# One streaming encoder layer: the scores matrix held in four places, reused by both projections, and PE alone in hand-written order in the down-projection

## The chip, the core and the metric

The kernel runs on one core of one Trainium2 chip. The metric is the device time of one execution in microseconds (us). TensorE (PE) does the matrix products, VectorE (DVE), ScalarE (ACT) and GpSimd (POOL) the work on elements, and SyncE (SP) issues most transfers; POOL issues the stores of intermediate results.

## What is computed

One layer of a streaming encoder for 2112 tokens (2048 of a prompt, 64 of a sample), width 1024, in fp32:

```
x = x + rms_norm(token_mixer(rms_norm(x)))        # gated convolution and mLSTM
x = x + rms_norm(memory_attend(rms_norm(x)))      # 4 heads, 256 memory tokens
x = x + rms_norm(conv_ffn(rms_norm(x)))

def conv_ffn(xn, ff_buf, w_up, ffn_conv_w, w_down):
    up, ff_new = causal_dwconv(xn @ w_up, ff_buf, ffn_conv_w)
    a, g = jnp.split(up, 2, axis=-1)
    return (jax.nn.gelu(g) * a) @ w_down, ff_new
```

`w_up` is 1024 x 5632 and `w_down` 2816 x 1024. The gains of the norms are folded into operands where that is possible.

## The kernel before

Every fp32 operand of a product is split into a high part, cast by ACT to the matrix format (L103), and a low part, which DVE subtracts (L104); `split` does both. A product of two operands is then three products on PE (`mm3`, L117 high by high, L118 and L119 with one low part). A profile row of line 103 or 104 is thus named by its tile alone.

The program has five phases. Phases 1 and 2 are the token mixer. Phase 3 is the attention: the weights of queries and keys are multiplied into one scores matrix `A`, those of values and output into `B`, both kept in SBUF with high and low parts. Tokens come in 16 chunks of 128 (and the sample's 64): scores `sc` from `A`, softmax `pp`, transposes into `ps`, then `yo` from `B`, the post-norm (`post`, L553) to `yn`, and the transpose of the next norm's input (`x2_T`, tiles `xr` and `tp`, L1238), stored as `x2T`.

Phase 4 is the up-projection, a Strassen-Winograd form with seven products instead of eight. Tokens come in three passes of two column blocks of 352, and each pass goes over 22 values of f: 66 units. A unit has seven products of four pairs (84 instructions of PE): the weights `wa`, `wb`, `wc`, `wd` (partly sums made earlier and kept in `wsd`) by the token operands B11, T2, B21, T1, T3, T4, B22, which DVE makes from the four quarters R11, R12, R21, R22 of `x2T`; X is R22 - R12 after R12 has become R12 - R11. `head1` is the first product of a unit, `head2` the second. Results are convolved, passed through gelu and stored by POOL as `hd`.

Phase 5 is the down-projection in six parts of 3, 3, 4, 4, 4, 4 blocks of 128 rows of `w_down`. A part loads and splits its weights (`load_down`: tiles `raw`, then `dh` and `dl`), and goes over nine groups of tokens, of 256 (one of 64): `load_h` loads `hr` from `hd` and splits it to `hh`, one group ahead (`need(i + 1)`), PE makes `y`, and DVE adds it to the accumulator of its tile `acc`. In the last part each tile of 128 tokens also gets the post-norm: two squares on ACT, a multiplication by the gain on POOL, small steps `poss`, `pov`, `por`, the addition of the residual `xt` (L570), and two stores `out_y`, which SP issues.

The order of instructions on an engine is either the scheduler's or that of the program. In phases 3 to 5 PE and SP have the order in which the code is written (`self.ms`), in the last part of phase 5 ACT, DVE and POOL too. SP issues in its order, and a transfer that must wait for a buffer or a result holds back those behind it. `raw` has three buffers; `hr`, `hh` and `xt` have two each.

Of the kernel before, what the change touches and what calls it, by code (L numbers as in the profile page):

```python
# [35 lines left out]
HEAD = 120  # L36
# [31 lines left out]
class Prog:  # L68
# [68 lines left out]
    def build(self):  # L137
        tc, nc = self.tc, self.nc
        with ExitStack() as es:
# [35 lines left out]
            self.pe = mybir.EngineType.PE  # L175
            self.zes = es.enter_context(ExitStack())
# [803 lines left out]
    def phase3(self):  # L980
# [4 lines left out]
        ap = self.pool(self.zes, "za").tile([P, 2, KT, D], F32R, name="A")  # L985
        bp = self.pool(self.zes, "zb").tile([P, 2, KT, D], F32R, name="B")
        A = lambda part, k, sl: ap[:, part, k, sl]
        B = lambda part, k, sl: bp[:, part, k, sl]
        with ExitStack() as es:
# [203 lines left out]
            for i in range(16):  # L1193
# [17 lines left out]
                if i + 1 < 16:  # L1211
                    pT(ch[i + 1])
                next(y)
# [28 lines left out]


    def phase4(self):
# [11 lines left out]
        KH = KT // 2  # L1256
        self.zes.close()
        self.zes = ExitStack()
        with ExitStack() as es:
# [6 lines left out]
            def t_op(n):  # L1266
                pool = right if n in ("T3", "B21") else left
                return pool.tile([P, KH, 2, NB], F32R, tag=n, name=n, bufs=1)

            def t_raw(n):  # L1270
                return left.tile([P, KH, NB], F32, tag=n, name=n, bufs=1)

            def w_op(n, bufs=1):
                return left.tile([P, 2, 2, KH, P], F32R, tag=n, name=n, bufs=bufs)


            ops = {n: t_op(n) for n in ("B11", "T2")}
            raws = {n: t_raw(n) for n in ("R11", "R12", "R21", "R22")}
            first = {n: w_op(n) for n in ("wa", "wb")}
            X = early.tile([P, KH, NB], F32, tag="X", name="X", bufs=1)  # L1280
# [9 lines left out]
            def w_load(u, part=("wa", "wb"), w=None):  # L1290
# [3 lines left out]
                if "wa" in part:  # L1294
                    w = W()
                    w.u, w.r = u, {}
                    w.r["wa"] = self.raw(a["w_up"][f], (P, KT, P)).rearrange("p (two k) c -> p two k c", two=2)
                if "wb" not in part:
                    return w
# [3 lines left out]
                w.r["wd"] = right.tile([P, KH, P], F32, tag="wr1", name="wr1", bufs=2)  # L1303
# [4 lines left out]
            def w_split(w, n):  # L1308
                if w is None:
                    return  # L1310
                if n == "wd":
                    o = left.tile([P, 2, KH, P], F32R, tag="wd", name="wd", bufs=1)
                else:
                    o = first.pop(n, None)
                    if o is None:
                        o = w_op(n, 2 if n == "wc" else 1)
                self.split(o[:, 0], o[:, 1], w.r[n])
                w.o[n] = o

            class Tk:  # L1320
                pass

            def t_load(p):
                t = Tk()
                t0 = 2 * NB * p
                t.r = raws if p == 0 else {n: t_raw(n) for n in ("R11", "R12", "R21", "R22")}
                t.w = None
                for n in ("R11", "R21", "R12", "R22"):
                    k0, c0 = (int(n[1]) - 1) * KH, t0 + (int(n[2]) - 1) * NB
                    self.dma(t.r[n], self.x2T[k0:k0 + KH, :, c0:c0 + NB].rearrange("k p t -> p k t"))  # L1330
                    if p == 0 and t.w is None:
                        t.w = w_load(0, ("wa",))
                t.o = {}
                t.X = X if p == 0 else None
                return t

            def t_split(p, t, n, src):
                o = ops[n] if p == 0 and n in ops else t_op(n)
                self.split(o[:, :, 0], o[:, :, 1], src)
                t.o[n] = o  # L1340

            def t_adds(t):
                V.tensor_tensor(out=t.r["R12"], in0=t.r["R12"], in1=t.r["R11"], op=ALU.subtract)
                if t.X is None:
                    t.X = early.tile([P, KH, NB], F32, tag="X", name="X", bufs=1)
                V.tensor_tensor(out=t.X, in0=t.r["R22"], in1=t.r["R12"], op=ALU.subtract)

            def t_t3(t):
                V.tensor_tensor(out=t.r["R11"], in0=t.X, in1=t.r["R11"], op=ALU.subtract)

            def t_t4(t):
                V.tensor_tensor(out=t.r["R21"], in0=t.r["R21"], in1=t.X, op=ALU.subtract)

            def prod(pt, w, n, i, o, more=False):
                h, l = (w.o[n][:, j] if i is None else w.o[n][:, j, i] for j in range(2))
# [47 lines left out]
            def head1(u, w, o):  # L1403
# [5 lines left out]
                v.p1 = vt("p1")  # L1409
# [10 lines left out]
            tk = t_load(0)  # L1420
            w = w_load(0, ("wb",), tk.w)
            with tc.high_priority(offset=HEAD):
                w_split(w, "wa")
                t_split(0, tk, "B11", tk.r["R11"])
                t_adds(tk)
                t_split(0, tk, "T2", tk.X)
            v = head1(0, w, tk.o)
            t_split(0, tk, "B21", tk.r["R21"])
            w_split(w, "wb")
            head2(v, tk.o)  # L1430
            t_split(0, tk, "T1", tk.r["R12"])
# [258 lines left out]
```

## Time and profile before

| | |
|---|---|
| median of 3 runs | 2946.56 us (2938.88 to 2947.24) |
| the profiled execution's own time | 2947.28 us |
| its span, first to last instruction | 2945.6 us |
| mean granted clock of PE | 0.989 |
| busy: PE, DVE, ACT, POOL | 2846.5, 1716.3, 1206.6, 378.0 us |
| instructions of PE | 15906 |

The span is what the rows of the trace cover; the time of an execution has 1.7 us around it. The median differs from the profiled execution by 0.7 us. A busy share is a mean over phases that have different limits, so the stretches around each change of phase have to be read by themselves.

### The profile page before, as it was taken

How to read it: one execution, taken by the hardware profiler on the slowest of the kernel's cores; microseconds unless marked ns; L12 is line 12 of the kernel's file. 1: busy time of each engine (PE TensorE's matmuls, PEld its weight loads, DVE VectorE, ACT ScalarE, POOL GpSimd, SP SyncE). 2: the span in 40 equal slices, each digit the busy share in tenths (PEclk: the TensorE clock that was granted, in tenths of full speed). 3: DMA queues.
4: the chain of work that ended last, by engine and by line, in shares of the span. 5: the costliest groups of instructions: out<-in, count | busy, mean ns of one | idle time of the engine just before them, and what ended most of it. 6: DMA issues, size and time to landing. Idle time of an engine off the chain costs nothing.

```text
span 2945.6 us, 41739 instructions
## 1 busy us (share of the span) xinstructions
PE 2846.5 (97%) x15906; PEld 2628.0 (89%) x15906; DVE 1716.3 (58%) x2815; ACT 1206.6 (41%) x2463; POOL 378.0 (13%) x608
## 2 busy tenths in 40 slices
PE   8999999999999999999979999999999989999987
PEld 8999999998988877788779999999999988888875
DVE  6413422355666555666477778877877753443457
ACT  5224223234344443223256566656666653110122
POOL 1111011112212202222100000000000000000034
PEclk9999999999999999999989999999999999999998
DMA  8434332158666335777455544554454532221235
GB/s 277 149 98 134 99 112 94 57 159 278 219 206 219 127 108 172 235 257 241 152 176 201 168 157 167 194 173 157 156 174 154 174 109 82 84 73 45 82 120 164
DMA packets 211498, 456.84 MB, mean 155 GB/s; under 512 B 25414, under 2 KB 113672, under 8 KB 211298
## 3 DMA queue, kind: packets, MB, share of 16 engines
q1 hardware_dynamic: 180418, 346.14, 37.2%
q0 software_dynamic: 28720, 100.17, 8.9%
q10 hardware_dynamic: 2160, 7.87, 1.0%
q8 instruction: 125, 2.05, 0.3%
q14 instruction: 75, 0.61, 0.1%
HBM read 345.56 MB, written 108.54 MB: 154 GB/s over the span
## 4 chain that ended last, share of the span: by engine, by line
PE 51%; DVE 6%; DMA 4%; issue 2%; ACT 1%; SPq 1%; POOL 0%; DVEq 0%; POOLq 0%; ACTq 0%
PE up L117 10%; PE up L119 10%; PE up L118 10%; PE y L118 4%; PE y L119 4%; PE y L117 4%; DMA sums<-in_w_up 2%; DVE acc L570 1%; PE yo L117 1%; PE yo L118 1%; PE yo L119 1%; DMA hr<-hd 1%; PE sc L119 1%; PE sc L117 1%; PE sc L118 1%
## 5 line engine op out<-in xcount | busy, mean ns | idle before, releaser
L117 PE MATMUL y<-dh,hh 128*128 128x512 f32 x704 | 278.9, 396 | 20.5 <-ACT hh L103 15.4
L119 PE MATMUL y<-dh,hh 128*128 128x512 f32 x704 | 278.7, 396 | 2.4 <-DVE hh L104 2.3
L118 PE MATMUL y<-dl,hh 128*128 128x512 f32 x704 | 277.7, 394 | 2.4 <-DVE dl L104 2.4
L117 PE MATMUL mm<-xs,wh 128*128 128x384 f32 (+2 forms) x768 | 249.0, 324 | 10.3 <-ACT xs L109 7.5
L119 PE MATMUL mm<-xs,wl 128*128 128x384 f32 (+2 forms) x768 | 248.7, 324 | 1.0 <-DVE wl L104 1.0
L118 PE MATMUL mm<-xs,wh 128*128 128x384 f32 (+2 forms) x768 | 248.8, 324 | 0.0
L1589 DVE TENSOR_TENSOR acc<-y,acc 128x512 f32<-128x512 f32 x170 | 115.7, 689 | 179.8 <-PE y L119 176.9
L117 PE MATMUL up<-B,wa 128*128 128x352 f32 x528 | 172.5, 327 | 8.8 <-ACT wa L103 8.8
L117 PEld LDWEIGHTS y<-dh,hh 128*128 128x128 f32 x704 | 134.7, 191 | 51.1 <-ACT hh L103 17.9
L117 PE MATMUL up<-T,wb 128*128 128x352 f32 x528 | 172.4, 326 | 3.7 <-ACT wb L103 2.6
L119 PE MATMUL up<-B,wa 128*128 128x352 f32 x528 | 170.3, 323 | 3.2 <-DVE wa L104 3.2
L117 PE MATMUL mmb<-bh,xs 128*128 128x384 f32 (+1 forms) x512 | 173.4, 339 | 0.0
L119 PE MATMUL mmb<-bh,xs 128*128 128x384 f32 (+1 forms) x512 | 172.5, 337 | 0.0
L118 PE MATMUL mmb<-bl,xs 128*128 128x384 f32 (+1 forms) x512 | 172.4, 337 | 0.0
L118 PE MATMUL up<-T,wb 128*128 128x352 f32 x528 | 170.3, 322 | 2.0 <-DVE T L104 2.0
L103 ACT CAST hh<-hr 128x1024 fp32r<-128x1024 f32 (+3 forms) x54 | 49.4, 914 | 297.5 <-PE y L119 248.8
L118 PE MATMUL up<-B,wa 128*128 128x352 f32 x528 | 170.7, 323 | 0.1
L119 PE MATMUL up<-T,wb 128*128 128x352 f32 x528 | 169.7, 321 | 0.5 <-DVE wb L104 0.5
L119 PEld LDWEIGHTS y<-dh,hh 128*128 128x128 f32 x704 | 134.5, 191 | 33.5 <-DVE hh L104 5.6
L118 PEld LDWEIGHTS y<-dl,hh 128*128 128x128 f32 x704 | 134.5, 191 | 31.1 <-DVE dl L104 3.1
L76 POOL DMA_DIRECT2D hd<-da x88 | 47.5, 541 | 851.1 <-DVE da L1491 822.8
L117 PEld LDWEIGHTS mm<-xs,wh 128*128 128x128 f32 x768 | 145.8, 190 | 10.7 <-ACT xs L109 7.5
(462 smaller groups left out, 7853.4 us busy)
## 6 DMA issues: line engine op xcount, KB each, us to landing
ws<-wsd SPq DMA_DIRECT2D x132, 512.0 KB, 4.3
raw<-in_w_up SPq DMA_DIRECT2D x66, 512.0 KB, 5.4
raw<-in_wA SPq DMA_DIRECT2D x47, 512.0 KB, 3.6
sums<-in_w_up SPq DMA_DIRECT2D x176, 128.0 KB, 4.1
wsd<-sums POOLq DMA_DIRECT2D x44, 512.0 KB, 4.2
wr<-in_w_up SPq DMA_DIRECT2D x66, 256.0 KB, 4.6
xt<-in_x SPq DMA_DIRECT2D x32, 512.0 KB, 4.4
hr<-hd SPq DMA_DIRECT2D x32, 512.0 KB, 3.9
```

The lines of the kernel that those rows point to most:

```text
L76: self.nc.gpsimd.dma_start(out=out, in_=in_)
L103: nc.scalar.copy(hi, src)
L117: nc.tensor.matmul(out, lhsT=lh, rhs=rh, start=(first and i == 0), stop=False, skip_group_check=more)
L118: nc.tensor.matmul(out, lhsT=lh, rhs=rl, start=False, stop=False, skip_group_check=more)
L119: nc.tensor.matmul(out, lhsT=ll, rhs=rh, start=False, stop=(last and i == n - 1), skip_group_check=more)
L570: nc.vector.scalar_tensor_tensor(out=yn[:w, sl], in0=yn[:w, sl], scalar=r[:w, 0:1], in1=xt[:w, sl], op0=ALU.mult, op1=ALU.add)
L1589: V.tensor_tensor(out=acc[j][:, sl], in0=pt, in1=acc[j][:, sl], op=ALU.add)
```

## The change

The scores matrix `A` is four tiles of [128, 2, 2, 1024] instead of one, in a pool of its own (`za`) that stays open to the end of the kernel. Their four places are used again twice. In phase 4 they hold `Z0` to `Z3`: B11 and T2 in split form with the high and low parts of `wa`, the four quarters, X (in two pieces, three and one of its four blocks) and p1. In phase 5 they hold the weights: parts 0, 2 and 4 in A2 and A3, the others in A0 and A1, and `hh5`, the first group's `hh`, in A0.

`head4`, called in the loop of phase 3, issues the loads of R11, of the first raw weights and of R12, R22, R21 after the last scores, and later in two steps the splits of `wa` and R11, the subtractions, and the split of T2. `head5`, called in the last three units of phase 4, loads and splits the first weights of the down-projection and its first group. Phase 5 no longer stands in `self.ms`; it has a manual order for PE alone, and in the last part still one for ACT, DVE and POOL. The weights of the next part are loaded ahead of `need(i)` in the loop. `wr1` has one buffer instead of two.

```
@@ phase 3
-        ap = self.pool(self.zes, "za").tile([P, 2, KT, D], F32R, name="A")
+        self.za = self.pool(self.zaes, "za")
+        ap = [self.za.tile([P, 2, 2, D], F32R, tag="A%d" % i, name="A%d" % i, bufs=1) for i in range(4)]
...
+                if i == 14:
+                    self.head4(0)
                 y = yout(ch[i])
                 next(y)
+                if i == 14:
+                    self.head4(1)
...
+                if i == 15:
+                    self.head4(2)
                 next(y)
+    def head4(self, step):
+        nc, V = self.nc, self.nc.vector
+        if step == 0:
+            z = [self.za.tile([P, 4 * D], F32R if i < 2 else F32, tag="A%d" % i, name="Z%d" % i, bufs=1) for i in range(4)]
...
+            self.t_load4(0, ("R11",))
+            self.w4 = self.raw(self.a["w_up"][0], (P, KT, P)).rearrange("p (two k) c -> p two k c", two=2)
+            self.t_load4(0, ("R12", "R22", "R21"))
+        elif step == 1:
+            o = self.ops4["B11"]
+            self.split(self.wa4[0], self.wa4[1], self.w4)
+            self.split(o[:, :, 0], o[:, :, 1], self.raw4["R11"])
+        else:
+            self.t_adds4()
+            o = self.ops4["T2"]
+            for x, ks in self.X4:
+                self.split(o[:, ks, 0], o[:, ks, 1], x)
@@ phase 4
-                w.r["wd"] = right.tile([P, KH, P], F32, tag="wr1", name="wr1", bufs=2)
+                w.r["wd"] = right.tile([P, KH, P], F32, tag="wr1", name="wr1", bufs=1)
...
+            def head5(step):
+                if step == 0:
+                    self.dn = self.load_down(0, ("A2",), 0, 2)
...
+                    self.dma(self.hr5.rearrange("p (f t) -> p f t", f=PARTS[0]),
+                             self.hd[0:PARTS[0], :, 0:2 * P].rearrange("f p t -> p f t"))
+                else:
+                    t = self.za.tile([P, 4 * D], F32R, tag="A0", name="hh5", bufs=1)
...
+                    self.split(self.hh5[:, 0], self.hh5[:, 1], self.hr5.rearrange("p (f t) -> p f t", f=PARTS[0]))
+                    self.dn += self.load_down(0, ("A3",), 2)
...
+                if u == len(units) - 3:
+                    head5(0)
...
                 w_split(n, "wc")
+                if n is None:
+                    head5(1)
@@ phase 5
             with ExitStack() as self.ms:
                 self.phase3()
                 self.phase4()
-                self.phase5()
+            self.phase5()
...
+            es.enter_context(tc.manual_schedule(engines={self.pe}))
...
-            with tc.high_priority(offset=HEAD):
-                need(0)
-                ws = {0: load_down(0, 0, PARTS[0])}
+            hs[0] = self.hh5
+            ws = {0: self.dn}
...
+                if t0 == groups[3] and pi + 1 < len(PARTS):
+                    ws[pi + 1] = self.load_down(pi + 1, ("A2", "A3") if pi % 2 else ("A0", "A1"))
...
                 need(i)
                 need(i + 1)
-                if t0 == groups[3] and pi + 1 < len(PARTS):
-                    ws[pi + 1] = load_down(pi + 1, f0s[pi + 1], PARTS[pi + 1])
```

The order of PE and of POOL is the same in both kernels. Three places on other engines differ as follows. The first is ACT from phase 3 into phase 4: L560 (before) and L561 are the squares of the post-norm, L1128 (before) and L1130 the square for `xr`, B11 and Z0, T2 and Z1 the split operands. Before:

```order
L560 ACTIVATE pp_13084,poss_13556<-yo3_13531 128x512
L1128 ACTIVATE xr_13476,ss2_13569<-yn3_10175 128x1024
L560 ACTIVATE pp_13288,poss_13642<-yo3_13576 128x512
L560 ACTIVATE pp_13288,poss_13642<-yo3_13601 128x512
L1128 ACTIVATE xr_13628,ss2_13655<-yn3_10175 128x1024
L1367 COPY ca_13749<-halo_13693 128x2
L1367 COPY cg_13835<-halo_13693 128x2
L1367 COPY ca_13891<-halo_13693 128x2
L103 CAST B11_13684<-R11_13686 128x4x352
L103 CAST wa_13690<-raw_13697 128x1024
L103 CAST B21_13731<-R21_13688 128x4x352
L1410 COPY p1_13729<-up_13716 128x352
```

In the changed kernel, over the same squares (the casts of B11 and `wa`, here of `Z0`, stand four and three rows above the first one shown):

```order
L103 CAST ps3_13290<-tp_13541 128x512
L103 CAST Z1_13480<-Z2_13481 128x3x352
L561 ACTIVATE pp_13087,poss_13573<-yo3_13548 128x512
L103 CAST Z1_13480<-Z3_13482 128x352
L1130 ACTIVATE xr_13489,ss2_13586<-yn3_10178 128x1024
L561 ACTIVATE pp_13291,poss_13666<-yo3_13593 128x512
L561 ACTIVATE pp_13291,poss_13666<-yo3_13625 128x512
L1130 ACTIVATE xr_13652,ss2_13679<-yn3_10178 128x1024
L1430 COPY Z3_13482<-up_13716 128x352
L103 CAST B21_13730<-Z3_13482 128x4x352
L103 CAST wb_13733<-ws_13710 128x1024
```

The casts of B11 and `wa` have moved ahead of the squares of the last two chunks and the two casts of T2 between them; that of B21 still follows the last square (`xr_13652`), now behind the copy of p1 (L1430, which writes Z3).

The second is SP's queue from phase 4 into phase 5: `raw` are weights of the down-projection and `hr` groups of `hd`. Before:

```order
L73 DMA wr_22448<-in_w_up 128x512
L73 DMA hr<-hd 128x3x256
L73 DMA raw<-in_w_down 128x1024 x3
L73 DMA hr<-hd 128x3x256 x3
L73 DMA raw<-in_w_down 128x1024 x3
L73 DMA hr<-hd 128x3x256 x3
```

In the changed kernel:

```order
L73 DMA wr_22319<-in_w_up 128x512
L73 DMA raw<-in_w_down 128x1024 x2
L73 DMA hr_22330<-hd 128x3x256
L73 DMA raw<-in_w_down 128x1024 x5
L73 DMA hr<-hd 128x3x256 x2
```

Two weight tiles now stand ahead of the first group's `hr`, and five more between it and those of the next groups.

The third is SP's queue in the last part: `out_y<-acc` with the tile's number behind it are the stores of a tile (the first is 22831 before, 22715 after), `xt` the residual of a later tile, `hr` a group. Before:

```order
L73 DMA hr<-hd 128x4x256
L73 DMA xt_25400<-x2d 128x1024
L73 DMA out_y<-fo_25382 64x512 x2
L73 DMA xt_25444<-x2d 128x1024
L73 DMA out_y<-acc_22831 128x512 x2
L73 DMA hr<-hd 128x4x256
L73 DMA xt_25493<-x2d 128x1024
L73 DMA out_y<-acc_22832 128x512 x2
L73 DMA xt_25537<-x2d 128x1024
L73 DMA out_y<-acc_22833 128x512 x2
L73 DMA hr<-hd 128x4x256
L73 DMA xt_25586<-x2d 128x1024
```

In the changed kernel:

```order
L73 DMA hr<-hd 128x4x256 x4
L73 DMA out_y<-fo_25215 64x512 x2
L73 DMA xt_25277<-x2d 128x1024
L73 DMA out_y<-acc_22715 128x512 x2
L73 DMA xt_25326<-x2d 128x1024
L73 DMA hr<-hd 128x4x256
L73 DMA out_y<-acc_22716 128x512 x2
L73 DMA xt_25370<-x2d 128x1024
L73 DMA out_y<-acc_22717 128x512 x2
L73 DMA xt_25419<-x2d 128x1024
L73 DMA hr<-hd 128x4x256
L73 DMA out_y<-acc_22718 128x512 x2
```

Between the loads of `hr` stand two tiles' stores in either order, but before the change two such loads stand ahead of the first stores in this last part, and after it four (the row with x4 is the row ahead of `out_y<-fo`), so that each later load stands four tiles of stores earlier.

## Rows read from the trace of the kernel before

**Rows 1.** The waits of PE, whole kernel: us in total, times, longest.
```profile
PE y L117 <- ACT hh L103: 15.4, 6, 4.1
```

**Rows 2.** Windows by stretch: busy us (instructions) of each engine, granted clock, DMA.
```profile
1479.00:1505.00 26.00, 11.54 (x38) 9.71 (x38) 20.48 (x21) 14.67 (x19) 2.73 (x5) 0.67 0.37 123
2300.00:2390.00 90.00, 90.00 (x564) 90.00 (x564) 68.20 (x93) 54.27 (x124) 6.44 (x12) 1.00 0.37 122
2420.00:2800.00 380.00, 380.00 (x1678) 314.63 (x1678) 150.39 (x188) 70.14 (x86) 0.00 (x0) 1.00 0.24 73
```

**Rows 3.** Timeline of PE, phase 3 into 4: start, us, instruction, [idle before <-releaser].
```profile
1475.27 1.03 PE L1238 MATMUL tp<-ident,xr 128*128 128x128 f32 x8
...
1478.65 0.39 PE L119 MATMUL yo<-B,ps 128*128 128x512 f32 x1
...
1487.87 0.66 PE L117 MATMUL up<-B,wa 128*128 128x352 f32 x1 [8.83 <-ACT wa L103]
...
1498.31 0.66 PE L117 MATMUL up<-T,wb 128*128 128x352 f32 x1 [2.63 <-ACT wb L103]
...
1504.99 0.32 PE L117 MATMUL up<-T,wc 128*128 128x352 f32 x1
```

**Rows 4.** DMA issues: tiles, count, size, median us from issue to landing.
```profile
raw<-in_w_down SPq DMA_DIRECT2D x22, 512.0 KB, 5.7
...
R<-x2Td SPq DMA_DIRECT2D x12, 704.0 KB, 9.7
...
hr<-hd SPq DMA_DIRECT2D x16, 384.0 KB, 3.3
```

**Rows 5.** Timeline of ACT in the same stretch.
```profile
1483.00 1.06 ACT L1128 ACTIVATE xr<-yn 128x1024 f32<-128x1024 f32 x1 [3.17 <-DVE yn L570]
```

**Rows 6.** Timeline of DVE in the same stretch.
```profile
1473.32 0.75 DVE L1130 TENSOR_SCALAR xr<-yn,r2r 128x1024 f32<-128x1024 f32 x1 [0.75 <-POOL r2r L97]
...
1486.91 1.63 DVE L104 TENSOR_TENSOR B<-R,B 128x1408 fp32r<-128x1408 f32 x1 [1.04 <-ACT B L103]
```

**Rows 7.** Timeline of PE, phase 4 into 5.
```profile
2395.18 0.32 PE L119 MATMUL up<-B,wc 128*128 128x352 f32 x1
...
2400.62 0.80 PE L117 MATMUL y<-dh,hh 128*128 128x512 f32 x1 [5.12 <-ACT dh L103]
...
2403.76 0.80 PE L118 MATMUL y<-dl,hh 128*128 128x512 f32 x1 [2.35 <-DVE dl L104]
...
2409.38 0.39 PE L119 MATMUL y<-dh,hh 128*128 128x512 f32 x1
```

**Rows 8.** Timeline of SP's queue, phase 4 into 5.
```profile
2392.86 14.38 SPq L73 DMA_DIRECT2D hr<-hd  x3
```

**Rows 9.** Timeline of DVE in the last part.
```profile
2823.57 1.99 DVE L104 TENSOR_TENSOR hh<-hr,hh 128x1024 fp32r<-128x1024 f32 x1 [0.15 <-ACT hh L103]
...
2835.23 0.15 DVE L95 TENSOR_SCALAR pov<-poss 128x1 f32<-128x1 f32 x1
...
2840.05 1.22 DVE L104 TENSOR_TENSOR hh<-hr,hh 128x1024 fp32r<-128x1024 f32 x1 [4.66 <-ACT hh L103]
...
2850.94 0.16 DVE L95 TENSOR_SCALAR pov<-poss 128x1 f32<-128x1 f32 x1
...
2920.30 1.23 DVE L104 TENSOR_TENSOR hh<-hr,hh 128x1024 fp32r<-128x1024 f32 x1 [4.93 <-ACT hh L103]
```

**Rows 10.** Timeline of SP's queue, then of ACT, in the last part.
```profile
2850.20 0.39 SPq L73 DMA_DIRECT2D hr<-hd  x1
...
2855.06 1.04 ACT L103 CAST hh<-hr 128x1024 fp32r<-128x1024 f32 x1 [6.70 <-DMA hr<-hd]
```

**Rows 11.** Timeline of DVE, then of ACT, late in phase 4.
```profile
2341.97 0.69 DVE L104 TENSOR_TENSOR wd<-wr,wd 128x512 fp32r<-128x512 f32 x1 [2.18 <-ACT wd L103]
...
2356.32 1.05 ACT L103 CAST wa<-raw 128x1024 fp32r<-128x1024 f32 x1 [0.16 <-PE up L119]
```

**Rows 12.** Timeline of POOL in the last part.
```profile
2842.77 3.22 POOL L564 TENSOR_TENSOR acc<-acc,gpost 128x512 f32<-128x512 f32 x2 [6.70 <-ACT junk L560]
```

More of the change, by code (lines that the diff above doesn't have):

```diff
@@ L1266, in t_op @@
             def t_op(n):
+                if n in self.ops4:
+                    return self.ops4[n]
                 pool = right if n in ("T3", "B21") else left
                 return pool.tile([P, KH, 2, NB], F32R, tag=n, name=n, bufs=1)
-            def t_raw(n):
-                return left.tile([P, KH, NB], F32, tag=n, name=n, bufs=1)
             def w_op(n, bufs=1):
[L1274 to L1280, printed above, removed]
+                t = left.tile([P, 2, 2, KH, P], F32R, tag=n, name=n, bufs=bufs)
+                return t[:, 0], t[:, 1]
+            raws = self.raw4
             halo = right.tile([P, 2 * NF, 2], F32, name="halo")
@@ L1312, in w_split @@
                     o = left.tile([P, 2, KH, P], F32R, tag="wd", name="wd", bufs=1)
+                    o = o[:, 0], o[:, 1]
                 else:
[L1314 to L1317, printed above, removed]
+                    o = self.wa4 if n == "wa" else w_op(n, 2 if n == "wc" else 1)
+                self.split(o[0], o[1], w.r[n])
                 w.o[n] = o
-            class Tk:
-                pass
@@ L1323, in t_load @@
[L1323 to L1335, printed above, removed]
@@ L1348, in t_t3, with t_split, t_t2 @@
[L1348 to L1352, printed above, removed]
+            def t_split(t, n, src):
+                t[n] = o = t_op(n)
+                self.split(o[:, :, 0], o[:, :, 1], src)
+            def t_t2(t):
+                t["T2"] = o = t_op("T2")
+                for x, ks in self.X4:
+                    self.split(o[:, ks, 0], o[:, ks, 1], x)
@@ L1354, in prod, with t_t3, t_t4 @@
+            def t_t3():
+                for x, ks in self.X4:
+                    V.tensor_tensor(out=raws["R11"][:, ks], in0=x, in1=raws["R11"][:, ks], op=ALU.subtract)
+            def t_t4():
+                for x, ks in self.X4:
+                    V.tensor_tensor(out=raws["R21"][:, ks], in0=raws["R21"][:, ks], in1=x, op=ALU.subtract)
             def prod(pt, w, n, i, o, more=False):
-                h, l = (w.o[n][:, j] if i is None else w.o[n][:, j, i] for j in range(2))
+                h, l = (w.o[n][j] if i is None else w.o[n][j][:, i] for j in range(2))
@@ L1470, in phase4 @@
                 if last:
[L1471 to L1473 removed]
+                    t_split(nt, "T3", raws["R11"])
+                    t_t4()
+                on = nt if last else o
                 vn = head1(u + 1, n, on) if n else None
@@ L1505, in phase4, with load_down @@
         self.qes.close()
+    def load_down(self, pi, tags, lo=0, hi=None):
+        f0, nf = sum(PARTS[:pi]), PARTS[pi]
+        ws = []
+        for i in range(lo, nf if hi is None else hi):
+            if i % 2 == 0:
+                t = self.za.tile([P, 2, 2, D], F32R, tag=tags[(i - lo) // 2], name="dh", bufs=1)
+            raw = self.raw(self.a["w_down"][f0 + i])
+            self.split(t[:, i % 2, 0], t[:, i % 2, 1], raw)
+            ws.append((t[:, i % 2, 0], t[:, i % 2, 1]))
+        return ws
     def phase5(self):
@@ L1521, in phase5 @@
             junk = ev.tile([P, 512], F32, name="junk5")
-            def load_down(pi, f0, nf):
-                ws = []
-                pool = w1 if pi % 2 else w0
-                for i in range(nf):
-                    raw = self.raw(a["w_down"][f0 + i])
-                    wh = pool.tile([P, D], F32R, tag="h%d" % i, name="dh", bufs=1)
-                    wl = pool.tile([P, D], F32R, tag="l%d" % i, name="dl", bufs=1)
-                    self.split(wh, wl, raw)
-                    ws.append((wh, wl))
-                return ws
             def load_h(f0, nf, t0):
```

98 lines of the change are left out of this document (50 added, 48 removed).

## The prediction

> **What bounds the kernel now.** I read the waits of TensorE (PE) first, because it is the busiest engine, then the stretches at the three places where its largest waits of the up- and down-projection fall. Three sums stand out: 15.4 us in six pieces where the down-projection waits for ScalarE's (ACT) cast of `hh` [rows 1], one piece of 8.83 us for `wa` at the start of the up-projection [rows 3], and one of 5.12 us for `dh` at the start of the down-projection [rows 7]. Away from those places PE is the bound: in [rows 2] it is busy for all of 2300 to 2390 and of 2420 to 2800 at full clock, with 90.0/564 = 0.160 us for a product of the up-projection and 380.0/1678 = 0.2265 us for one of the down-projection. Nothing done to another engine in those stretches moves the end unless it makes PE wait. So the change is worth what it gives back at three places, less what it newly delays.
>
> Around a restart the waits are not the whole loss. The clock granted from 1479 to 1505 is 0.67 [rows 2], so products run at the lower of the two levels (1.2 GHz rather than 2.4 GHz) for some time after PE has stood still. I therefore price each place by the time from the last product before it to the first one after it that is undisturbed, less the products in between at full rate.
>
> **First place, scores to up-projection.** The last product of phase 3 starts at 1478.65 (so its successor could start at 1478.88), the first of `up` at 1487.87, the second weight block at 1498.31, and the third block at 1504.99 [rows 3]. Between 1478.88 and 1504.99 lie 36 products, 36 x 0.160 = 5.8 us; 20.3 us are lost. The changed kernel issues the loads of R11, of the first weights and of R12, R22, R21 as soon as the last product of scores has read the matrix, with the output products of two chunks still to come, 48 each, 2 x 48 x 0.2265 = 21.7 us, against a median landing of 9.7 us [rows 4]. B11, T2 and `wa` are then ready when PE gets there, and the first 12 products follow without a wait.
>
> What is not gained: the next 12 need B21, and in the order of ACT (shown with the change) its cast stands behind the square of the last chunk and a copy of p1. That square runs at 1483.00 for 1.06 us [rows 5], 5.2 us after 1478.88 at its end. The copy of 352 columns and the cast of 1408 are, at the square's 1.06 us for 1024, an estimated 0.4 and 1.5 us, so B21's high part is there 7 to 8 us after the end of phase 3, and its low part (1.63 us on VectorE (DVE) [rows 6]) 1.6 us later, about 9.5. PE has then stood for some 7 us, so 23 products (11 of B21, 12 of T2) run at first at the low rate, 20 of them at about twice 0.160 us less what the faster end of the stretch saves, 6.1 us in all, to the third block: 15.6 us after phase 3's end. The same instant now lies 26.1 us after it. Gain 10.5 us.
>
> Against that, the added work sits ahead of the last two chunks on DVE: two low parts, two subtractions and the split of T2, 1.63 + 1.22 + 3 x 1.6 = 7.7 us by [rows 6] and [rows 9], of which all but the last pieces, about 5.7 us, come ahead of the chain that ends in `xr` at 1473.32 + 0.75 [rows 6]; PE takes that tile for its transposes at 1475.27 without waiting [rows 3], 1.2 us later. That cover and the 0.75 us that DVE idles ahead of `xr` take up 2 us; other idle pieces of the chain may take up the rest: phase 3 ends 0 to 4 us later, I take 2.5. **Gain 8 us**, between 2 (4 us of delay, and T2 late as well) and 12 (no delay).
>
> **Second place, up- to down-projection.** The last `up` starts at 2395.18, the first `y` at 2400.62, the second at 2403.76, and the fifteenth, where full rate is back, at 2409.38 [rows 7]. 14 x 0.2265 = 3.2 us of work lies in 2409.38 - 2395.34 = 14.0: 10.8 us are lost. The first weights and `hh` now come during the last three units, and ACT and DVE have the room (in [rows 2] DVE is busy 68.2 and ACT 54.3 of 90 us). What is late next is the `hh` of the second group: needed 36 x 0.2265 = 8.15 us after 2395.34, at 2403.5 (its low part at 2403.95). On SP its load stands behind seven loads of weights, the last of which needs a buffer that is free only after a split at about 2395.5; the load then issues near 2396 and takes 3.3 us or a little more [rows 4], and its cast stays behind ACT's last work on `da`, which the added cast of `dh` pushes back by some 2.5 us, because its raw tile takes 5.7 us to land [rows 4]. I get 2401.3 to 2402.5 for the high part, 2403.3 to 2405 for the low one: a wait of 0 to 1 us. **Gain 9.5 us**, between 4 and 10.8.
>
> **Third place, the last part of the down-projection.** There DVE works in blocks of one group: a low part of `hh` starts at 2840.05 and the block ends at 2850.94 + 0.16 = 2851.10, which is 11.05 us; the next low part does not follow until the next group's cast, and the last of the six repeats starts at 2920.30 [rows 9]. (2920.30 - 2840.05)/5 = 16.05 us: 5.0 us of each repeat are idle. What ends them is the load: ACT's cast at 2855.06 waited 6.70 us for the transfer of `hr`, which SP issued at 2850.20 [rows 10]. In SP's hand-written order that load stands behind the `out_y` pairs of the group before. In the new order (shown with the change) the same load stands ahead of four more tiles of output, over 20 us earlier, so it has landed long before. DVE's block then sets the pace: it beats PE's 48 x 0.2265 = 10.9 us. The low part of the third group can start where its predecessor's block ends, 2835.23 + 0.15 = 2835.4 instead of 2840.05, and the last one at 2835.4 + 5 x 11.05 = 2890.6 instead of 2920.30. That is 29.7 us; **gain 29.5 us**. Lower bound: if each of six low parts takes 1.99 us as at 2823.57 instead of 1.22 [rows 9], 25. Upper: 31, if the first group gains too.
>
> **Costed at nothing.** The one buffer of `wr1` (two before): its load now waits for the low part of `wd`, until 2341.97 + 0.69 = 2342.7, and with it the raw weights behind it on SP, which ACT casts at 2356.32 [rows 11]. At a landing of 5.7 us they are there by 2348.4, 8 us before; if that cover were gone, each of 64 units would pay the excess. Splitting X in two adds some twelve DVE instructions and three casts in three pass changes; at full cover nothing, without it under 2 us. I deduct 0.3. The order of PE and of GpSimd (POOL) is the same row by row.
>
> **Sum.** 8 + 9.5 + 29.5 - 0.3 = 46.7 us. From the profiled execution's own 2947.28 us that gives 2900.6; the median of the runs shown lies 0.7 us lower: 2900 us, with a span near 2899.
>
> **A rule against it.** In the last part POOL multiplies for 3.22 us per tile [rows 12], and the row at 2823.57 shows a low part at 1.99 us where the one at 2840.05 takes 1.22 [rows 9]. The Trainium skill, "SBUF — State Buffer", section "Who interferes with whom", says that a VectorE instruction with two SBUF inputs and a GpSimd one that reads SBUF exclude each other for the whole instruction. The trace agrees in direction, with 1.99 us beside 1.22. By the rule, were every low part to meet a multiply and wait it out, the sum would be 35.4 us instead of 46.7.
>
> **Rivals.**
> *POOL collision.* Each of seven low parts waits out one multiply (3.22/2 = 1.6 us): 29.5 - 11.3, so about 2911 us. For it: low parts now start when POOL has long been idle, and the change moves them to the end of a block. Against it: POOL's multiply of the block's first tile ends at 2842.77 + 3.22 = 2845.99 [rows 12], before the small results that close that tile, and the second runs in the same rhythm, so that POOL is through when the next low part begins. One in ten. This is the mechanism that the section named above would make of it.
> *The second group is late at the start of the down-projection.* If the seven weight loads hold SP for longer than I reckon, PE waits up to 8 us there and pays the low clock again: the second gain is gone, 2910 us. For it: today three loads of `hr` hold SP for 14.38 us right there [rows 8], since buffers are missing. Fifteen in a hundred.
> *The last part keeps its pace.* If the load of `hr` finds its own buffer taken, or `xt` takes its place as the late transfer, 0 to 5 us remain of 29.5: 2925 to 2929 us. Against it: the buffer is freed by a low part two groups earlier. One in ten.
> *Slower.* The single `wr1` buffer makes PE wait in each unit: to end 0.3% above before it must cost (46.7 + 8.8)/64 = 0.87 us per unit, that is, SP's wait must exceed its cover of 8 us by that much. The times in [rows 11] leave it well short, but loads of `ws` stand on the same queue. Four in a hundred.
>
> **How the numbers follow.** My forecast gets 0.61, with 2890 to 2907 for its own bounds, from the sums of the bounds taken half together. Adding collision and late group takes the range to 2911 and part of the unmoved tail: 2887 to 2922. About 0.3% (9 us) is what a measurement of this kernel tells from no change; the case between, several losses at once that leave under 9 us, gets 0.03.
>
> **What would show it.** Right: `up` starts within 1 us of the last `yo`, then a wait of about 7 us for B21; `y` follows `up` without a gap; low parts of `hh` in the last part 11 us apart, the sum of waits for `hh` near nothing. Wrong: PE waits spread over the units for `wa` or `wd`; a gap over 3 us some 8 us into the down-projection; low parts still 16 us apart, or 12 to 13 with each one longer; or phase 3's last products more than 4 us later relative to its start.

## The result, and the profile after

The changed kernel takes 2900.14 us (median of 4 runs, 2897.68 to 2903.74), the kernel before 2943.83 us (4 runs, 2938.88 to 2947.24): a ratio of 0.9854, 95% interval 0.9834 to 0.9874. The forecast was 2900 us. The profiled execution took 2897.68 us, with a span of 2895.9 us (2945.6 before); it is the fastest of its four, that of the kernel before the slowest of its four. One execution in this study, of 3129.25 us in the kernel with the load moved, ran at a mean granted clock of 0.847 instead of 0.992 and is left out of its median.

PE's share rises to 98%, though it is busy for 14 us less, in line with a mean granted clock of 0.994 instead of 0.989: fewer products run at the low clock. The page's first part and PE's longest waits of the changed kernel (in total, times, longest):

```profile
PE 2832.6 (98%) x15906; PEld 2622.4 (91%) x15906; DVE 1717.6 (59%) x2827; ACT 1204.7 (42%) x2466; POOL 384.0 (13%) x608
```

```profile
PE tp L1246 <- DVE xs L104: 13.2, 8, 4.8
PE up L117 <- ACT B L103: 9.2, 1, 9.2
...
PE up L117 <- ACT u L1486: 3.2, 5, 1.3
...
PE y L119 <- DVE hh L104: 0.2, 1, 0.2
```

The 15.4 us of [rows 1] are gone, and so are the waits for `wa` and `dh` at the starts of the two projections; one wait of 9.2 us, for B21 (here `B`), has come in their place. PE's timeline from phase 3 into 4, which answers to [rows 3], and the windows of the three places, which answer to the first row of [rows 2] (first column after the stretch: its length, then PE's busy time; the third number from the end is the granted clock):

```profile
1474.63 0.39 PE L119 MATMUL yo<-B,ps 128*128 128x512 f32 x1
1474.86 0.32 PE L117 MATMUL up<-Z 128*128 128x352 f32 x1
...
1486.12 0.66 PE L117 MATMUL up<-B,Z 128*128 128x352 f32 x1 [9.19 <-ACT B L103]
1487.78 0.66 PE L118 MATMUL up<-B,Z 128*128 128x352 f32 x1 [1.00 <-DVE B L104]
...
1492.90 0.32 PE L117 MATMUL up<-T,wc 128*128 128x352 f32 x1
```

```profile
1475.00:1501.00 26.00, 15.81 (x88) 15.15 (x87) 18.13 (x21) 15.74 (x23) 1.82 (x4) 0.80 0.47 161
2385.70:2400.00 14.30, 14.30 (x65) 11.87 (x64) 9.17 (x11) 8.53 (x14) 2.15 (x4) 1.00 0.85 269
2798.20:2895.90 97.70, 87.22 (x385) 71.88 (x383) 90.16 (x111) 32.28 (x76) 66.22 (x49) 0.97 0.64 202
```

`up` follows the last `yo` at once. After 12 products PE stands for 9.19 us, and the clock falls (products of 0.66 us behind the wait, 0.32 ahead of it; 0.80 on average over the 26 us). The down-projection begins without a gap (2385.64 the last `up`, 2385.80 the first `y`) and at full clock. In the last part DVE's low parts of `hh` are 11.0 us apart:

```profile
2815.67 1.22 DVE L104 TENSOR_TENSOR hh<-hr,hh 128x1024 fp32r<-128x1024 f32 x1
...
2826.67 1.23 DVE L104 TENSOR_TENSOR hh<-hr,hh 128x1024 fp32r<-128x1024 f32 x1
...
2837.66 1.22 DVE L104 TENSOR_TENSOR hh<-hr,hh 128x1024 fp32r<-128x1024 f32 x1
```

**Where the time went.** PE executes the same 15906 products in the same order in all kernels of this study, so the same product can be found in each trace. The stages below run between the starts of five of them: the last `yo`, the first product of the third weight block of `up`, the last `up`, the fifteenth `y`, the first `y` of the last part's first full group, the last `y`; then to the end of the span. All in us, each from the profiled execution.

| kernel | last `yo` to third block | to last `up` | to 15th `y` | to last part | last part | to the end |
|---|---|---|---|---|---|---|
| before | 26.34 | 890.18 | 14.21 | 408.48 | 115.49 | 12.22 |
| changed | 18.28 | 892.74 | 3.34 | 409.24 | 86.81 | 10.92 |
| difference | -8.1 | +2.6 | -10.9 | +0.8 | -28.7 | -1.3 |

These sum to -45.6 of the 49.6 us between the spans. The other 4.0 us lie ahead of the last `yo`, at 1478.65 and 1474.63. Some 5 us belong to one stretch of phase 3 where the kernel before waited 3.00 us for `xs` at 1407.95 and then ran at the low clock (0.76 granted from 1408 to 1415), which the experiments show to come and go by itself; smaller differences go the other way, among them 0.6 us by which the last `yo` comes later after the last `sc`, 0.40 of it a wait for `xr` at the last transposes. By the ratio, over all runs, the change is worth 43 us.

### The profile page after: what moved, and what is told of

Same layout as the page of the kernel before. It is cut to its first block, busy times and chain, and to the rows that moved or that the text cites. A ratio compares the mean times of both kernels' runs of the same rounds, so it can differ in the third digit from the quotient of the medians.

```text
span 2895.9 us, 41744 instructions
## 1 busy us (share of the span) xinstructions
PE 2832.6 (98%) x15906; PEld 2622.4 (91%) x15906; DVE 1717.6 (59%) x2827; ACT 1204.7 (42%) x2466; POOL 384.0 (13%) x608
## 4 chain that ended last, share of the span: by engine, by line
PE 43%; DVE 5%; issue 1%; ACT 1%; DMA 0%; DVEq 0%; POOLq 0%; POOL 0%; ACTq 0%
PE up L117 10%; PE up L118 10%; PE up L119 10%; PE y L119 5%; PE y L117 4%; PE y L118 4%; DVE acc L571 1%; DVE acc L1623 1%; DVE poss L566 1%; DVE T L104 0%; PE y L129 0%; PE y L128 0%; DVE B L104 0%; DVE da L1411 0%; DVE Z L104 0%
## 5 line engine op out<-in xcount | busy, mean ns | idle before, releaser
L119 PE MATMUL y<-dh,hh 128*128 128x512 f32 x704 | 274.2, 389 | 0.2 <-DVE hh L104 0.2
L118 PE MATMUL y<-dh,hh 128*128 128x512 f32 x704 | 273.9, 389 | 0.0
L117 PE MATMUL y<-dh,hh 128*128 128x512 f32 x704 | 273.9, 389 | 0.0
L119 PEld LDWEIGHTS y<-dh,hh 128*128 128x128 f32 x704 | 132.1, 188 | 28.5 <-DVE hh L104 1.2
L118 PEld LDWEIGHTS y<-dh,hh 128*128 128x128 f32 x704 | 132.1, 188 | 27.5
L117 PEld LDWEIGHTS y<-dh,hh 128*128 128x128 f32 x704 | 132.1, 188 | 27.2
L117 PEld LDWEIGHTS mm<-xs,wh 128*128 128x128 f32 x768 | 146.7, 191 | 10.0 <-ACT xs L109 7.9
L119 PEld LDWEIGHTS mm<-xs,wl 128*128 128x128 f32 x768 | 146.7, 191 | 1.9 <-DVE wl L104 1.9
L118 PEld LDWEIGHTS mm<-xs,wh 128*128 128x128 f32 x768 | 146.6, 191 | 0.6 <-DVE xs L110 0.4
L1411 DVE SCALAR_TENSOR_TENSOR da<-ca,cst,da 128x704 f32<-128x704 f32 (+1 forms) x132 | 125.5, 951 | 9.2 <-ACT da L1409 7.1
L1411 DVE SCALAR_TENSOR_TENSOR dg<-cg,cst,dg 128x704 f32<-128x704 f32 (+1 forms) x132 | 125.2, 948 | 6.8 <-ACT dg L1409 1.4
L104 DVE TENSOR_TENSOR bl<-braw,bh 128x384 fp32r<-128x384 f32 (+1 forms) x80 | 41.7, 558 | 135.6 <-ACT bh L103 135.6
L103 ACT CAST wh<-raw 128x1024 fp32r<-128x1024 f32 (+1 forms) x49 | 50.5, 1031 | 158.4 <-PE mm L118 121.3
```

What stands on the lines that cost most here:

```text
L103: nc.scalar.copy(hi, src)
L104: (eng or nc.vector).tensor_tensor(out=lo, in0=src, in1=hi.bitcast(F32), op=ALU.subtract)
L117: nc.tensor.matmul(out, lhsT=lh, rhs=rh, start=(first and i == 0), stop=False, skip_group_check=more)
L118: nc.tensor.matmul(out, lhsT=lh, rhs=rl, start=False, stop=False, skip_group_check=more)
L119: nc.tensor.matmul(out, lhsT=ll, rhs=rh, start=False, stop=(last and i == n - 1), skip_group_check=more)
L1411: V.scalar_tensor_tensor(out=d[:, :e], in0=c[:, i:e + i], scalar=w[i], in1=d[:, :e], op0=ALU.mult, op1=ALU.add)
```

## The experiments

**The last part: the place of `hr` in SP's queue.** Two kernels, from both sides. In the first, the changed kernel, SP is in hand-written order:

```
-            es.enter_context(tc.manual_schedule(engines={self.pe}))
+            es.enter_context(tc.manual_schedule(engines={self.pe, mybir.EngineType.SP}))
```

> The changed kernel with SP too in hand-written order in the down-projection. Theory, that the place of the loads of hr in SP's queue sets the pace of the last part: low parts of hh go back from 11.0 to about 16 us apart there, six repeats x 5 us, so about 29 us slower than the changed kernel, near 2929 us; the two earlier places stay as they are, within 2 us. Rival, that the last part gained from the new places of the weights or from the order of the other engines: within 4 us of the changed kernel.

In the second, the kernel before, only the transfer is issued ahead (`load_r` is the first half of `load_h`):

```
                 need(i)
                 need(i + 1)
+                if last and i + 2 < len(work):
+                    rs[i + 2] = load_r(f0s[pi], PARTS[pi], work[i + 2][1])
```

> The kernel before, with one edit: in the last part the load of hr is issued one group earlier in SP's hand-written order, everything else as it was. Theory: low parts of hh come about 11 us apart and 28 to 30 us are saved, near 2915 us, with nothing of the scheduler's order needed. Rival, that the scheduler's order as a whole (xt and out_y moved as well) makes the gain: under 5 us.

The kernel with SP in written order took 2920.38 us, 0.9932 of the kernel before (0.9912 to 0.9951). Its last part is 114.75 + 13.65 us long to the end of the span, where the changed kernel takes 86.81 + 10.92; its stages from the last `yo` to the last part are the changed kernel's within 1 us. The whole is 20 us slower than the changed kernel and not 29, at least in part because the stages ahead of the last `yo` were shorter: it starts 7.0 us earlier in this execution. The cast of `hh` waits for its transfer as in [rows 10]. ACT's timeline of this kernel:

```profile
2828.74 1.04 ACT L103 CAST hh<-hr 128x1024 fp32r<-128x1024 f32 x1 [6.78 <-DMA hr<-hd]
...
2844.99 1.04 ACT L103 CAST hh<-hr 128x1024 fp32r<-128x1024 f32 x1 [6.89 <-DMA hr<-hd]
```

The kernel with the load moved took 2905.30 us (median of three), 0.988 (0.9862 to 0.9897). Its last part is 86.81 + 10.92 us, the changed kernel's to the hundredth, and its stages from the last `yo` to there are the kernel before's within 1 us. (Ahead of them this execution is 12.7 us shorter than the profile of the kernel before, by no edit: its last `yo` starts at 1465.94.) DVE's low parts and SP's loads in it:

```profile
2822.96 1.22 DVE L104 TENSOR_TENSOR hh<-hr,hh 128x1024 fp32r<-128x1024 f32 x1
...
2833.95 1.23 DVE L104 TENSOR_TENSOR hh<-hr,hh 128x1024 fp32r<-128x1024 f32 x1
```

```profile
2822.08 0.44 SPq L73 DMA_DIRECT2D hr<-hd  x1
...
2833.12 0.39 SPq L73 DMA_DIRECT2D hr<-hd  x1
```

So the place of one transfer in SP's queue is the whole of the last part's 30 us; one group of lead is enough, and nothing else of the scheduler's order is needed.

**The second place: early weights and `hh`.** The changed kernel without `head5`:

```
-                if u == len(units) - 3:
-                    head5(0)
...
-                if n is None:
-                    head5(1)
...
-            hs[0] = self.hh5
-            ws = {0: self.dn}
+            ws = {0: self.load_down(0, ("A2", "A3"))}
```

> The changed kernel without the early start of the down-projection: its first weights and first hh are loaded and split where phase 5 begins, in the same places. Theory, that the early loads and splits make the gain at the second place: PE waits again for hh and dh for some 5 to 8 us and then runs at the low clock, 9 to 11 us slower than the changed kernel, near 2910 us. Rival, that the scheduler's freedom in SP's order would bring these loads forward anyway: within 3 us of the changed kernel.

It took 2900.71 us, 0.9867 (0.985 to 0.9884), where the changed kernel has 0.9854: by its median no loss can be told. The trace does show one, in this stage alone: 12.74 us from the last `up` to the fifteenth `y` instead of 3.34. PE's timeline of this kernel:

```profile
2384.34 0.80 PE L117 MATMUL y<-dh,hh 128*128 128x512 f32 x1 [4.42 <-ACT hh L103]
...
2387.06 0.79 PE L119 MATMUL y<-dh,hh 128*128 128x512 f32 x1 [1.50 <-DVE hh L104]
```

The scheduler brought the weights forward (the waits for `dh` did not return), the first `hh` not: by `head5` 9.4 us are gained, as the first theory had it, and half of the rival is right too. What hides it are the stages ahead of the last `yo`, which vary by as much from execution to execution; in this profile the last `yo` starts at 1469.16, 5.5 us ahead of the changed kernel's.

**The first place: early loads and splits.** The changed kernel with `head4` called where phase 4 starts:

```
-                if i == 14:
-                    self.head4(0)
...
+            for st in range(3):
+                self.head4(st)
```

> The changed kernel with the three steps of head4 all called at the start of phase 4, so that the loads of the quarters and of the first weights are issued only behind phase 3's. Theory, that the early issue and the splits ahead of the end of phase 3 make the first place's gain: the gain of 7 us turns into a loss, since the loads are now later than in the kernel before as well (landing 10 us): 8 to 20 us slower than the changed kernel, 2908 to 2920 us, and the first up waits over 9 us. Rival, that the four places alone free SBUF early enough: within 3 us. The steps ahead of row 1404 of PE's timeline also tell whether the 4.6 us that the changed kernel was ahead there belong to the change.

It took 2898.16 us, 0.9858 (0.9839 to 0.9877): by its median neither slower nor faster than the changed kernel. Its trace does show a loss. Executions differ by some 5 us ahead of this place, so that times have to be counted from a product that all of them execute, here the last `sc` of phase 3. That product and the issue of the load of R11, in the kernel before (`R`), in the changed kernel (`Z`) and in this one:

```profile
1454.21 0.39 PE L119 MATMUL sc<-A,xs 128*128 128x512 f32 x1
1458.61 0.43 SPq L73 DMA_DIRECT2D R<-x2Td  x1
```

```profile
1449.60 0.39 PE L119 MATMUL sc<-A,xs 128*128 128x512 f32 x1
1448.66 0.38 SPq L73 DMA_DIRECT2D Z<-x2Td  x1
```

```profile
1444.94 0.39 PE L119 MATMUL sc<-A,xs 128*128 128x512 f32 x1
1449.33 0.43 SPq L73 DMA_DIRECT2D Z<-x2Td  x1
```

The load is issued 4.4 us after the last `sc` here, exactly as in the kernel before, and 0.9 us ahead of it in the changed kernel. B11's cast follows 11.5 us after the last `sc`, 3.6 in the changed kernel. It still runs well inside phase 3, since the four places are free by then and engines that are not in hand-written order take the work up. But the splits now end only just ahead of the last chunks' `xr`. DVE's last subtraction and `xr`, in the changed kernel and then in this one:

```profile
1465.81 0.51 DVE L1368 TENSOR_TENSOR Z<-Z,Z 128x352 f32<-128x352 f32 x1
...
1470.31 0.75 DVE L1132 TENSOR_SCALAR xr<-yn,r2r 128x1024 f32<-128x1024 f32 x1 [0.75 <-POOL r2r L97]
```

```profile
1468.18 1.25 DVE L1365 TENSOR_TENSOR Z<-Z 128x1056 f32<-128x1056 f32 x1
1469.89 0.75 DVE L1132 TENSOR_SCALAR xr<-yn,r2r 128x1024 f32<-128x1024 f32 x1 [0.46 <-POOL r2r L97]
```

That is 20.7 and 25.0 us after the last `sc` for `xr` (19.1 in the kernel before). PE's timeline of this kernel:

```profile
1470.79 1.69 PE L1240 MATMUL tp<-ident,xr 128*128 128x128 f32 x8 [4.63 <-DVE xr L1132]
...
1486.39 0.66 PE L117 MATMUL up<-B,Z 128*128 128x352 f32 x1 [8.25 <-ACT B L103]
```

PE waits 4.63 us for `xr` there, 0.40 in the changed kernel, and the clock falls: from the last `sc` to the last `yo` it needs 30.9 us, 25.0 in the changed kernel and 24.4 in the kernel before. From the last `yo` to the third block it needs 17.58, a little less than the changed kernel. From the last `sc` to the third block that makes 50.8 us before the change, 43.3 with it and 48.5 here. So of the 7.5 us at this place, 5.2 come with the calls inside phase 3, by the early issue and splits that the theory names; the other 2.3 are there without them. The loss of 8 to 20 us that was expected did not come, because the loads are not later than in the kernel before. The rival fails too: the places alone do not do it. These 5.2 us as well are below what the medians can tell.

**The wait for B21.** ACT's timeline of the changed kernel behind the last square:

```profile
1480.03 0.43 ACT L1430 COPY Z<-up 128x352 f32<-128x352 f32 x1
1484.70 1.36 ACT L103 CAST B<-Z 128x1408 fp32r<-128x1408 f32 x1 [4.24 <-issue]
```

The cast is next in ACT's order, its source is long there, and it starts 4.2 us late for nothing that the profile names. POOL issued the store of phase 3's last `yn` at 1479.88, and such stores land in a median of 4.7 us:

```profile
1479.88 0.58 POOL L76 DMA_DIRECT2D x2d<-yn  x1 [2.39 <-DVE yn L571]
```

```profile
x2d<-yn POOLq DMA_DIRECT2D x16, 512.0 KB, 4.7
```

This one landed after 4.7 us too: 1479.88 + 4.7 = 1484.6. If B21 lies where phase 3's last tiles lay, it is the store that frees its place. Three kernels put other operands there (a first, a second and a third exchange):

```
-                pool = right if n in ("T3", "B21") else left
+                pool = right if n in ("T3", "T1") else left
...
+                pool = right if n in ("T4", "B22") else left
...
+                pool = right if n in ("T3", "B22") else left
```

> The changed kernel with the places of B21 and T1 exchanged: B21 where the attention's output matrix was, T1 where phase 3's last tiles were. In the changed kernel PE waited 9.19 us for B21, whose cast started 4.2 us after ACT's last work for nothing that the profile names. Theory, that this cast waits for the place of B21, free only when the store of phase 3's last chunk has landed: the cast follows the copy of p1 at once, PE's wait falls from 9.2 to about 5 us, and T1's cast now starts where B21's did, so that the third block begins some 3 us earlier. Rival, that the order of ACT behind the last square sets it: the wait stays above 8 us.

> As the exchange before, but with the two operands that are needed last, T4 and B22, in the place that comes free late, and B21, T1 and T3 all in the other. Theory (place): neither B21 nor T1 waits, PE's wait for B21 is about 5 us, and 3 to 5 us are saved against the changed kernel at the start of the up-projection, about 2896 us where that one gives 2900. Rival (order of ACT): no change.

> The changed kernel with T3 and B22 in the place that comes free late, B21 and T1 in the other. Theory (place of B21): the third block begins 3 to 4 us earlier after phase 3 than in the changed kernel, as with the two exchanges before; T3, needed 12 products after T1, waits for its place no longer than the rest of the chain does. Theory (places set a product's time): a mean that differs from 160.7 ns. Rival: 160.7 ns and no gain at the start.

The place holds in all: B21's cast follows the copy at once. ACT and PE of the first exchange:

```profile
1478.05 0.43 ACT L1430 COPY Z<-up 128x352 f32<-128x352 f32 x1
1478.38 1.37 ACT L103 CAST B<-Z 128x1408 fp32r<-128x1408 f32 x1
```

```profile
1479.80 0.66 PE L117 MATMUL up<-B,Z 128*128 128x352 f32 x1 [4.85 <-ACT B L103]
```

In the first exchange it is T1 that takes the late place. The store is issued at 1477.90 and lands 4.3 us later, at 1482.2, and T1's cast starts right behind it; the low part of B that the profile names for it had ended at 1481.41:

```profile
1482.34 1.36 ACT L103 CAST T<-Z 128x1408 fp32r<-128x1408 f32 x1 [1.56 <-DVE B L104]
```

PE's wait is 4.8 us in all three, and the third block comes 13.90, 14.90 and 15.15 us after the last `yo` instead of 18.28. The times: 2892.31 us (one run), 2893.48 (0.9852, 0.9836 to 0.9869) and 2891.0 (0.983, 0.9813 to 0.9847). The changed kernel, run again beside the first two, needs 2893.25:

> The changed kernel once more, beside the others on one chip: 2897 to 2904 us. It also shows whether the waits of phase 2 and of phase 3 ahead of the change, some 5 us each in some executions, come and go without any change of the kernel, and whether a product of the up-projection takes 160.7 ns again rather than the 160.0 ns of the kernel before.

That is 0.9846 (0.9831 to 0.9861) of the kernel before on that chip, 2937.94, and about the ratio of the first comparison. So the second exchange is no faster than the changed kernel though it starts 3 us sooner, and the third is faster by 0.16%, with intervals that overlap; a gain in the whole is not shown. From the third block to the last `up` the three need 893.75, 895.79 and 892.42 us, the changed kernel 892.74 and 893.45: the second exchange loses 2 to 3 us there again.

**What a product of the up-projection takes.** In windows of 200 us in the first pass, in which PE is busy throughout, the number of products behind PE's busy time differs: 1252 in the kernel before, 1247 in the changed one, 1243 with T4 and B22 in the late place (one row each, in this order):

```profile
1550.00:1750.00 200.00, 200.00 (x1252) 200.00 (x1251) 152.60 (x181) 120.39 (x223) 8.12 (x15) 1.00 0.54 180
```

```profile
1550.00:1750.00 200.00, 200.00 (x1247) 200.00 (x1246) 151.98 (x181) 118.08 (x222) 8.11 (x15) 1.00 0.50 176
```

```profile
1550.00:1750.00 200.00, 200.00 (x1243) 200.00 (x1242) 149.28 (x178) 119.73 (x225) 8.13 (x15) 1.00 0.45 163
```

By the starts of the products that is 160.00, 160.7 and 161.1 ns each, at the same granted clock of 1.00. The next kernel is the kernel before with only the places changed, as in the second exchange above:

> The kernel before with one edit: T4 and B22 in the place of T3 and B21 and the reverse. Nothing of the order of PE changes. So far a product of the up-projection took 160.00 ns in the kernel before, 160.7 in the changed kernel, 160.4 with B21 and T1 exchanged there and 161.1 with T4 and B22 in the late place. Theory, that the places of the operands in SBUF set it: the mean leaves 160.00 ns by 0.2 ns or more, one way or the other. Rival, that something else of the change sets it (the shared place of wa and B11, one buffer of wr1, the weights' arrival): 160.00 ns as before, and the up-projection's units 13.44 us.

One run gave 2943.53 us, beside 2941.5 for the kernel before. Its products take 160.24 ns on average (1250 in the same window), and not evenly: those of B21 and B22, two of the four operands that were moved, take 160.83 ns, those of the other five, the moved T3 and T4 among them, 160.00. In three executions with the places of the kernel before, all seven take 160.00. So the places take part in it, as far as one execution shows; that they do not settle it alone is told further below. The last version tried the fourth pair:

> As the one before, with T3 and T4 in the late place. The same gain of 3 to 4 us at the start of the up-projection; a mean time of a product that differs again if places set it, the same one if they don't. If it is at or under 160.4 ns, this version is 3 to 6 us faster than the changed kernel, near 2888 us beside 2893 on the same chip.

2890.54 us, 0.9831 (0.9811 to 0.985); its third block starts 14.15 us after the last `yo`, and its products take 160.4 ns, as those of the third exchange do. The 3 to 6 us against the changed kernel are not shown: that one was not run on this chip, and its 0.9846 lies inside the interval.

**One buffer for `wr1`.** The kernel before with `bufs=1` there:

> The kernel before with one buffer for wr1 instead of two, nothing else. Theory of the prediction, that the 8 us of cover absorb the later load: units stay at 13.44 us and the time within 3 us of the kernel before. Rival, the slower case of the prediction: waits for wa or wd in the units, 0.06 us or more in each of 64, 4 us or more in all; 0.06 us a unit would also account for the 2.3 us that the up-projection lost.

2940.55 us, 1.0007 (0.9998 to 1.0017) in 10 runs beside 13. The units last 13.44 us as before, from the third block to the last `up` 890.21 us beside 890.18, there is no wait for `wd`, and those for `wa` are the kernel before's: the slower rival's mechanism does not act there. In the changed kernel PE has no wait for `wd` either, and waits for `wa` (there `Z`) only at the two changes of pass, 0.51 us each, where the kernel before waits 1.36. Two buffers in the changed kernel were not tried.

## Why the prediction was right, and where it wasn't

Of the signs named, `up` right behind the last `yo`, `y` without a gap, low parts 11 us apart and almost no wait for `hh` came; the wait for B21 was 9.2 us and not about 7.

*Last part.* Forecast 29.5 us, measured 28.7 + 1.3 = 30.0 us, by the mechanism named, and both kernels that isolate it agree. Blocks of DVE take 11.0 us (11.05 forecast).

*POOL collision.* It did not come: low parts keep 1.22 us in the changed kernel. POOL's multiplication ahead of the low part of 2826.67 ends at 2826.53, just in time. The rule from the Trainium skill, "SBUF — State Buffer", "Who interferes with whom", by which the one of the two that comes second waits for the whole of the other's instruction, shows from the other side. POOL's `por` in the changed kernel, in turn without and with a low part on DVE:

```profile
2821.96 0.54 POOL L97 TENSOR_TENSOR por<-pov,small 128x1 f32<-128x1 f32 x1 [0.35 <-DVE pov L95]
...
2826.88 1.41 POOL L97 TENSOR_TENSOR por<-pov,small 128x1 f32<-128x1 f32 x1 [0.35 <-DVE pov L95]
```

The low part of 2826.67 began 0.2 us earlier and POOL's step ended 0.4 us after it; the trace agrees with the rule, and DVE, which came first, lost nothing. The same cost stands on the chain to `xr` in the kernel that calls `head4` late: POOL's `r2r`, 0.56 us in the changed kernel, takes 1.43 beside DVE's subtraction of 1468.18.

*Second place.* Forecast 9.5 us, measured 10.9. The step mis-sized is the `hh` of the second group: 0 to 1 us of waiting was reckoned, and there was none. SP issued its load at 2384.49, 1.2 us before the last `up`, and not 0.8 us after it; its cast ran at 2390.19 and its low part from 2392.10, for products at 2393.97 and 2394.42.

*First place.* Forecast 8, measured 7.5: 8.1 from the last `yo` on, less the 0.6 us ahead of it. The sum was right by luck, as two errors cancel. Phase 3 was to end 2.5 us later and ended 0.6 later: the work of the splits found idle time on DVE that the prediction did not count (2.61 and 4.50 us ahead of two multiplications for `yn`, at 1461.70 and 1468.09 in the kernel before). And B21's high part was to be there 7 to 8 us after phase 3, by ACT's order, where it came 11.2 us after. The step that failed is the sentence that ACT's order sets B21: a place that a store still holds set it, by 4.2 us. With B21 in another place its high part is there 6.9 us after phase 3, as the order alone would have it. That the early issue of the loads makes the gain held for 5.2 of the 7.5 us.

*Costed at nothing.* `wr1` was right (the 5.7 us taken for its landing are those of `w_down`; the weights of `w_up` land in a median of 5.4). That the up-projection would otherwise lose only 0.3 us was not: it lost 2.6. Of these, 0.65 us lie in the first units and at the two changes of pass, and 1.9 in the units between, where a product takes 0.7 ns longer in the first two passes and 0.2 ns less in the third. The change of places was not priced at all.

*The level.* The sum of 46.7 us stands beside 45.6 us by stages and 43.7 us by medians. It was taken from a median of 2946.56 us, 2.7 above that of the four runs compared, so that 2900 meets 2900.14 as closely as it does is luck too. The profiled execution read for it held some 5 us in phase 3 that come and go.

## What to carry to other kernels

Where an engine that issues transfers works in written order, look at what each load stands behind: here one load moved by one group was worth two thirds of the whole change. When a cast or a load starts late and the profile names no releaser, look for a store that still reads the tile's place, and give that place to the operand that is needed last (here this brought the third block 3 to 4 us forward; in the whole the gain is not shown). Before judging an edit of a few microseconds by medians, compare the stages between the same products in both traces: three effects of 3 to 9 us were clear there and not in the medians. Count from such a product and not from the start of the trace: by the clock of the traces R11's load seemed to be issued as early without the early calls (1449.33 and 1448.66), counted from the last `sc` it was 5.3 us later.

## What the runs showed of the hardware that was not expected

A product of 352 columns at full clock took 160.00 ns in the kernel before in all three passes, and 160.2 to 161.1 ns in kernels that differ in where the operands lie, with PE busy throughout and no wait recorded. It also differed within one kernel, with the same places: the changed one ran the units of the first two passes in 13.50 us (160.7 ns a product) and those of the third in 13.42 (159.8 ns). Run again it ran at 13.42 for four units of the second pass and at 13.50 behind a unit of 13.60 us, to the end; the kernel without `head5` had its second pass at 13.42, the one with `head4` late its third. So the place of an operand and something that a pause of PE can change both act on it. Which places are good, and what the pause changes, stays open; over the 5544 products of the up-projection it is worth, as an estimate, up to 6 us more than at 160.00 ns, or 1 us less.

Two stretches that no edit touches differed between executions: the one of phase 3 named above (between the starts of the 7500th and the 7845th product) took 76.7 us in the kernel before and 71.2 in the same code with the moved load, and one of phase 2 (3700th to 4200th) took 81.5 in the kernel before and in the changed one, and 76.1 to 80.7 in the others. What they wait for was not followed up.
